# An fp32 decoder trunk on one core: weight splits ahead of the transposes' evacuations, modulation steps placed elsewhere

## The chip, the cores and the metric

The kernel runs on one core of a Trainium2 chip. The metric is the device time of one execution in microseconds (us), the median over several; less is better.

## The reference

`x` (1 x 256 x 1024, fp32) passes two layers, each of a half-step gated FFN, a token mixer and a second half-step FFN. Each of the six sub-layers is wrapped in norms and a modulation that is itself a product with the condition `c`. Cut to what matters here:

```
for layer in range(2):
    mod = (silu(c) @ ada_w[layer] + ada_b[layer]).reshape(B, 3, 3, D)
    h = rms_norm(x, g[0, 0]) * (1 + scale) + shift          # from mod
    y = (silu(h @ w_in[:, :2816]) * (h @ w_in[:, 2816:])) @ w_out
    x = x + 0.5 * gate * rms_norm(y, g[0, 1])
    y = short_conv(h') if layer == 0 else nsa(h', shared keys and values)
    x = x + gate' * rms_norm(y, g[1, 1])
    y = swiglu_ffn(h'', ...);  x = x + 0.5 * gate'' * rms_norm(y, g[2, 1])
```

The short convolution is three column parts of `h @ w_in`, two of them multiplied, convolved over three tokens, multiplied by the third, then a product with `w_out`. The attention has three branches (compressed, selected and window keys) in 16 heads; its keys and values come once from `x` after the first layer. All products keep fp32 accuracy.

## The kernel before, in words

**A product.** A matmul in full fp32 is replaced by three in a rounded fp32 form: a weight w is split into `whi` (its rounded copy) and `wlo = w - whi`, the activations likewise, and `mm3` (L252 to 254) adds x_hi w_hi, x_hi w_lo and x_lo w_hi. The activations stand transposed in `hx`, 8 blocks of 128 rows by 256 tokens, in a high and a low part; `t` is the half of 128 tokens. `prod(name, t)` multiplies one half of the tokens by 512 columns of a weight in 24 matmuls, and `prod_out` multiplies columns that were evacuated and transposed (`H`) by the second weight, into the `y` banks.

**Weights.** Every weight comes through a fixed plan (`w_init`) of transfers of 1 MB on SP's queue into three `raw` buffers. Each transfer holds two units of 128 x 1024. `fwd(n, g)` splits the next n units of the plan: first n copies on ACT (`whi`, L149), then on DVE n subtractions (`wlo`, L155) with g modulation steps pumped in between. Split units lie in pool A (6 buffers) or pool B (4), which the plan chooses by a letter. A raw buffer's next transfer is issued when its last subtraction is. Where a product needs a unit not yet split, `unit` splits it on the spot.

**Modulation.** 160 steps (`g_step`, L208) each multiply 512 KB of `ada_w`, which come by SP's queue into three `graw` buffers, with silu(c) on DVE and add them up into a column of `mod`. `pump` makes the credit for them, `g_need` forces those that a sub-layer needs next, and `row_of` turns a finished row for the gate with transposes (L304).

**Stages.** Start; first FFN; convolution; second FFN; keys' phase (`kv_side`); third FFN; attention (`nsa`, with `heads`); fourth FFN; end. Each FFN begins with `ffn_head` and then runs over blocks of 256 hidden columns. Between two sub-layers `turn_over` finishes the output product, adds to x (`z`, `x`), normalises, transposes (L290) and writes the new `hx` (L358 to 368). Meanwhile it runs the next sub-layer's first product in four pieces, p0 to p3 (`pair`, `kv_first`, `q_first`): the first half of the tokens needs only the first half of `hx`, and half two's transposes stand between p1 and p2.

**Order.** The engines' queues take what the program writes, in its order; no scheduler moves anything. A transposition is a TensorE instruction into a `tr` bank behind the product in hand, and its evacuation (ACT copies such as `quarter`, `H`, `T`; DVE's low part) waits for it. So where `fwd` stands in the text against an evacuation decides when its copies start.

## Time and profile before

| | us |
|---|---|
| median of 3 runs (1124.12 to 1126.97) | 1126.36 |
| the profiled execution, its own time | 1124.14 |
| its span in the profile | 1122.4 |
| TensorE busy | 1055.5 (94%) |
| DVE busy | 778.3 (69%) |
| ACT busy | 529.2 (47%) |
| mean granted clock of TensorE | 0.976 |

PE is TensorE's matmul, PEld its weight load, SP the engine whose queue issues transfers. In a timeline a row gives the start and length in us, the engine, the line, the operation, output <- inputs, the shape and a count; in brackets stands how long the engine had waited and for what. In a view of busy time by stage a row gives the stretch from:to and its length, then the busy us and the count of PE, PEld, DVE, ACT and POOL, then TensorE's granted clock (1.00 is full), the busy share of the DMA engines and the GB/s that they moved. The stretches are cut at the first matmul of each stage.

### The profile page before, as it was taken

Reading aid. Unit: us, or ns where it says so; the run is one execution under the profiler, and the core shown is the slowest. Engines: PE = TensorE matmul, PEld = TensorE weight load, DVE = VectorE, ACT = ScalarE, POOL = GpSimd, SP = SyncE. Lnnn points to the kernel's source line nnn. Section 1 sums busy time; section 2 is a strip of 40 time slices with the busy share of each in tenths; the row PEclk is TensorE's granted clock in tenths of the full one; section 3 lists DMA queues with packets and bytes.
Section 4 is the critical chain, followed back from the end, with each engine's and each line's share of the span. In section 5 each row is a group of like instructions: output and inputs, shape, how many; then the busy total and the mean of one; then the engine's idle time right before and its main releaser. Section 6 shows DMA issues by size and latency. Waiting matters only on the chain. (4 is left out here: it accounts for less than half of the span.)

```text
span 1122.4 us, 13355 instructions
## 1 busy us (share of the span) xinstructions
PE 1055.5 (94%) x4862; PEld 840.0 (75%) x4862; DVE 778.3 (69%) x1348; ACT 529.2 (47%) x974; POOL 31.4 (3%) x84
## 2 busy tenths in 40 slices
PE   5999999997999999999978999999999979999997
PEld 3578888775777888887857888886787757888786
DVE  5688788857675777777467877785477776665553
ACT  3444444645464344446444434444478645344342
POOL 0000000100010000001100000001000010000000
PEclk9999999999998999999999999999889989999999
DMA  9988988645645888885655888885411255655541
GB/s 367 389 300 298 344 314 327 236 163 215 224 167 187 314 294 308 288 292 211 225 205 209 314 308 300 290 304 199 177 63 39 94 206 201 236 222 184 188 150 38
DMA packets 51089, 263.50 MB, mean 235 GB/s; under 512 B 5584, under 2 KB 8016, under 8 KB 30288
## 3 DMA queue, kind: packets, MB, share of 16 engines
q1 hardware_dynamic: 50640, 261.61, 64.2%
q0 software_dynamic: 384, 1.05, 0.4%
q8 instruction: 38, 0.62, 0.2%
q14 instruction: 27, 0.22, 0.1%
HBM read 260.54 MB, written 1.05 MB: 233 GB/s over the span
## 5 line engine op out<-in xcount | busy, mean ns | idle before, releaser
L252 PE MATMUL in<-whiA,hx 128*128 128x512 f32 x760 | 300.6, 395 | 7.2 <-ACT whiA L149 3.6
L253 PE MATMUL in<-wloA,hx 128*128 128x512 f32 x760 | 298.5, 393 | 8.1 <-DVE wloA L155 8.1
L254 PE MATMUL in<-whiA,hx 128*128 128x512 f32 x760 | 299.4, 394 | 0.0
L155 DVE TENSOR_TENSOR wloA<-raw,whiA 128x1024 fp32r<-128x1024 f32 x205 | 246.0, 1219 | 68.4 <-ACT whiA L149 68.4
L149 ACT ACTIVATE whiA<-raw 128x1024 fp32r<-128x1024 f32 x205 | 205.7, 1049 | 12.9 <-DMA raw<-in_wi_dram 5.3
L208 DVE SCALAR_TENSOR_TENSOR graw<-graw,sc 128x1024 f32<-128x1024 f32 x147 | 178.8, 1218 | 4.8 <-DMA graw<-in_ada_dram 4.7
L252 PEld LDWEIGHTS in<-whiA,hx 128*128 128x128 f32 x760 | 143.5, 189 | 40.7 <-ACT whiA L149 5.5
L253 PEld LDWEIGHTS in<-wloA,hx 128*128 128x128 f32 x760 | 143.6, 189 | 39.4 <-DVE wloA L155 10.5
L254 PEld LDWEIGHTS in<-whiA,hx 128*128 128x128 f32 x760 | 143.5, 189 | 34.6 <-DVE hx L362 4.9
L422 ACT ACTIVATE sg<-in 128x256 f32<-128x256 f32 x86 | 33.0, 383 | 272.7 <-PE in L254 272.6
L252 PE MATMUL y<-whiB,H 128*128 128x512 f32 x368 | 152.2, 413 | 1.4 <-ACT whiB L149 1.4
L253 PE MATMUL y<-wloB,H 128*128 128x512 f32 x368 | 146.0, 397 | 3.4 <-DVE wloB L155 3.4
L155 DVE TENSOR_TENSOR wloB<-raw,whiB 128x1024 fp32r<-128x1024 f32 x112 | 134.2, 1221 | 21.0 <-ACT whiB L149 21.0
L254 PE MATMUL y<-whiB,H 128*128 128x512 f32 x368 | 146.1, 397 | 0.8 <-DVE H L296 0.8
L149 ACT ACTIVATE whiB<-raw 128x1024 fp32r<-128x1024 f32 x112 | 112.2, 1052 | 0.7 <-DMA raw<-in_wo_dram 0.4
L423 DVE TENSOR_TENSOR ht<-in,sg 128x256 f32<-128x256 f32 x86 | 36.4, 424 | 109.2 <-ACT sg L422 109.1
L253 PEld LDWEIGHTS y<-wloB,H 128*128 128x128 f32 x368 | 70.3, 191 | 17.6 <-DVE wloB L155 5.1
L254 PEld LDWEIGHTS y<-whiB,H 128*128 128x128 f32 x368 | 70.1, 190 | 17.0 <-DVE H L296 1.9
L252 PEld LDWEIGHTS y<-whiB,H 128*128 128x128 f32 x368 | 70.2, 191 | 13.8 <-ACT whiB L149 1.7
L295 ACT ACTIVATE H<-tr 128x256 fp32r<-128x256 f32 x88 | 33.1, 382 | 97.3 <-PE tr L290 97.3
L296 DVE TENSOR_TENSOR H<-tr,H 128x256 fp32r<-128x256 f32 x88 | 36.6, 420 | 44.8 <-ACT H L295 44.8
L290 PE MATMUL tr<-sm,ht 128*128 128x128 f32 x192 | 36.5, 276 | 7.2 <-DVE ht L423 5.1
(209 smaller groups left out, 1023.5 us busy)
## 6 DMA issues: line engine op xcount, KB each, us to landing
raw<-in_wi_dram SPq DMA_DIRECT2D x84, 1024.0 KB, 6.5
graw<-in_ada_dram SPq DMA_DIRECT2D x147, 512.0 KB, 4.8
raw<-in_wo_dram SPq DMA_DIRECT2D x44, 1024.0 KB, 6.9
raw<-in_cv_dram SPq DMA_DIRECT2D x12, 1024.0 KB, 6.4
whiB<-in_ada_dram SPq DMA_DIRECT2D x8, 512.0 KB, 9.7
raw<-in_ao_dram SPq DMA_DIRECT2D x4, 1024.0 KB, 5.6
raw<-in_q_dram SPq DMA_DIRECT2D x4, 1024.0 KB, 6.5
raw<-in_w_dram SPq DMA_DIRECT2D x4, 1024.0 KB, 6.9
```

Of the source, the lines that this page charges most:

```text
L149: nc.scalar.activation(hi[:, :w], raw, AF.Copy)
L155: nc.vector.tensor_sub(lo, raw, hi.bitcast(F32))
L208: self.nc.vector.scalar_tensor_tensor(w, w, 1.0, self.sc, op0=OP.mult, op1=OP.mult, accum_out=self.mod[:, m, k:k + 1])
L252: mm(out, xh, wh, start=start, stop=False, skip_group_check=True)
L253: mm(out, xh, wl, start=False, stop=False, skip_group_check=True)
L254: mm(out, xl, wh, start=False, stop=stop, skip_group_check=True)
L290: self.nc.tensor.transpose(o[:, i * 128:i * 128 + 128], src[:, i * 128:i * 128 + 128], self.ident)
L295: self.nc.scalar.activation(h[0], src, AF.Copy)
L296: self.nc.vector.tensor_sub(h[1], src, h[0].bitcast(F32))
L422: nc.scalar.activation(sg, o[:, 0:256], AF.Silu)
L423: nc.vector.tensor_mul(ht, o[:, 256:512], sg)
```

## The change

It does seven things. (1) In `conv`, `ffn_head`, `kv_side` and `kv_block` the call of `fwd` stands ahead of the evacuation of transposes (`then`, `turn_in`) instead of behind it; two `conv` blocks split 3 and 3 units instead of 2 and 4. (2) `ffn_head` pumps no modulation steps any more; the FFNs' rates rise to 1.5 (0.45 in the last), attention's rate falls from 3.0 to 1.5, `q_first` pumps 2 and 3 steps, and `nsa` pumps none at its start and more behind the heads. (3) The plan gives the second FFN's first output weight ahead of its third input block, and some units other pools. (4) In `pair` and `kv_first` one unit instead of two stands ahead of the second half's transposes. (5) The turn-over into the keys' phase splits 1 and 4 units in its middle, not 1 and 2. (6) In `heads` the query products of the third block stand ahead of the loop, those of the fourth at heads 2 and 3. (7) Two splits move from heads 8 and 9 to 12 and 14, and two others behind the gates and compressed values.

```diff
-    G_FFN = (1.5, 1.2, 1.25, 0.35)
+    G_FFN = (1.5, 1.5, 1.5, 0.45)
-    G_ATT = 3.0
+    G_ATT = 1.5
...
-        ffn(1, False, "ABAB")
+        ffn(1, False, "ABAA")
-        ffn(2, False)
+        ffn(2, False, "AABA")
-        ffn(3, False, "BAAB")
+        ffn(3, False, "BAAA")
...
@@ def pair(self, name, evac):
-            o[1] = self.prod((*name, 1), 0, None, range(2))
+            o[1] = self.prod((*name, 1), 0, None, range(1))
-            self.prod((*name, 1), 0, o[1], range(2, 4))
+            self.prod((*name, 1), 0, o[1], range(1, 4))
...
@@ def ffn_head(self, n):
         o = self.prod(("wi", n, 1), 1)
+        self.fwd(2)
         self.turn_in(ht[0, 1], H[0], 1)()
-        self.fwd(2, g)
         ht[1, 1] = self.evac_in(o)
...
@@ def conv(self, nxt):
         for j in range(2, 6):
             o = self.prod(("cv", j), 0)
+            self.fwd(3 if j in (2, 3) else 2, g)
             then[j - 1, 1]()
-            self.fwd(2, g)
             evac(j, 0, o)
             o = self.prod(("cv", j), 1)
+            self.fwd(3 if j in (2, 3) else 2, g)
             then[j, 0]()
-            self.fwd(4 if j in (2, 3) else 2, g)
             evac(j, 1, o)
...
@@ def kv_block(self, e):
         b = self.proj(("kw", e))
+        self.fwd(2)
@@ def kv_side(self, first):
         self.then[0]()
-        self.fwd(2, g)
+        self.pump(g)
         o = self.prod(("vv",), 1)
+        self.fwd(2)
         self.kv_evac(0, 1, o)
...
@@ def q_first(self):
             o[2] = self.compress(0)
+            self.pump(2)
...
             o[3]()
+            self.pump(3)
...
@@ def heads(self):
         self.cmp_scores(0)
+        self.q_half(2, 0)
         soft_a(0)
...
         scores(2)
+        self.q_half(2, 1)
         bias(3)
...
-            if i < 4:
-                self.q_half(2 + i // 2, i % 2)
+            if i in (2, 3):
+                self.q_half(3, i - 2)
...
-            if i < 4 or 8 <= i < 10:
+            if i < 4 or i in (12, 14):
                 self.fwd(1)
...
@@ def nsa(self, nxt):
         then()
-        self.fwd(2, g)
         gates()
         self.cmp_values()
+        self.fwd(2)
         self.heads()
...
-        self.fwd(4, g / 2)
+        self.fwd(4, g)
         self.prod_out(1, rows(0, 4), True, False)
-        self.fwd(2, g)
+        self.fwd(2, 2 * g)
@@ def run(self):
-        self.ffn(1, 8, over(self.kv_first, 19, 18))
+        self.ffn(1, 8, over(self.kv_first, 19, 18, more=(1, 4)))
```

Line numbers after the change are four to six lower for the same statement (L149 becomes L145, L155 becomes L151, L208 becomes L204).

ACT's queue in the convolution, around its third column block; `quarter<-tr` and `H<-quarter` evacuate transposes, `whiA` and `whiB` are weight copies. Before:

```order
L530 ACTIVATE sg<-in 128x256
L539 ACTIVATE quarter<-tr 128x2x128
L544 ACTIVATE z<-quarter,sm 128x256 x2
L149 ACTIVATE whiA<-raw 128x1024 x2
L552 ACTIVATE quarter<-in 128x512
L295 ACTIVATE H<-quarter 128x2x128 x2
L149 ACTIVATE whiB<-raw 128x1024 x2
L149 ACTIVATE whiA<-raw 128x1024 x2
```

After:

```order
L525 ACTIVATE sg<-in 128x256
L145 ACTIVATE whiA<-raw 128x1024 x2
L145 ACTIVATE whiB<-raw 128x1024
L534 ACTIVATE quarter<-tr 128x2x128
L539 ACTIVATE z<-quarter,sm 128x256 x2
L547 ACTIVATE quarter<-in 128x512
L145 ACTIVATE whiB<-raw 128x1024
L145 ACTIVATE whiA<-raw 128x1024 x2
L291 ACTIVATE H<-quarter 128x2x128 x2
```

The weight copies, three units per product instead of two and four, now stand ahead of the evacuation that needs the transposes.

ACT's queue in the head of the second FFN; `sg<-in` evacuates a product, `H<-tr` transposes. Before:

```order
L422 ACTIVATE sg<-in 128x256
L295 ACTIVATE H<-tr 128x2x128 x2
L149 ACTIVATE whiA<-raw 128x1024 x2
L422 ACTIVATE sg<-in 128x256
L295 ACTIVATE H<-tr 128x2x128
L149 ACTIVATE whiB<-raw 128x1024 x2
L422 ACTIVATE sg<-in 128x256
L295 ACTIVATE H<-tr 128x2x128
```

After:

```order
L418 ACTIVATE sg<-in 128x256
L145 ACTIVATE whiB<-raw 128x1024 x2
L291 ACTIVATE H<-tr 128x2x128 x2
L418 ACTIVATE sg<-in 128x256
L145 ACTIVATE whiA<-raw 128x1024 x2
L291 ACTIVATE H<-tr 128x2x128
L418 ACTIVATE sg<-in 128x256
L145 ACTIVATE whiA<-raw 128x1024 x2
L291 ACTIVATE H<-tr 128x2x128
```

The B copies that the first output product needs (`whiB`) moved from behind the second evacuated pair to the front, and each pair of copies ahead of its `H<-tr`.

DVE's queue behind attention, up to the turn-over's normalisation (`z<-x`); `graw` rows are modulation steps. Before:

```order
L155 TENSOR_TENSOR wloB<-raw,whiB 128x1024
L208 SCALAR_TENSOR_TENSOR graw,mod<-graw,sc 128x1024
L155 TENSOR_TENSOR wloB<-raw,whiB 128x1024
L208 SCALAR_TENSOR_TENSOR graw,mod<-graw,sc 128x1024 x3
L221 TENSOR_TENSOR mod<-mod,sm 128x8
L229 SCALAR_TENSOR_TENSOR mod<-mod,sm 128x8
L208 SCALAR_TENSOR_TENSOR graw,mod<-graw,sc 128x1024
L221 TENSOR_TENSOR mod<-mod,sm 128x8
L331 TENSOR_TENSOR z<-y,g 128x512 x2
L337 SCALAR_TENSOR_TENSOR x<-z,sty_7366,x 128x512 x2
L331 TENSOR_TENSOR z<-y,g 128x512
L345 TENSOR_SCALAR z<-x,stx_7401 128x512 x2
```

After:

```order
L151 TENSOR_TENSOR wloB<-raw,whiB 128x1024
L204 SCALAR_TENSOR_TENSOR graw,mod<-graw,sc 128x1024
L217 TENSOR_TENSOR mod<-mod,sm 128x8
L151 TENSOR_TENSOR wloB<-raw,whiB 128x1024
L204 SCALAR_TENSOR_TENSOR graw,mod<-graw,sc 128x1024 x2
L151 TENSOR_TENSOR wloB<-raw,whiB 128x1024
L327 TENSOR_TENSOR z<-y,g 128x512 x2
L333 SCALAR_TENSOR_TENSOR x<-z,sty_7372,x 128x512 x2
L327 TENSOR_TENSOR z<-y,g 128x512
L341 TENSOR_SCALAR z<-x,stx_7407 128x512 x2
```

Before, four forced steps stand directly ahead of the first `z<-y,g`, with the finishing of two rows (L221, L229) among them; now two pumped ones and a low half stand there, and the rows are finished earlier.

## Rows read from the trace of the kernel before

**Rows 1.** The page's busy shares, costliest groups (busy us, mean ns) and DMA issues

```profile
PE 1055.5 (94%) x4862; PEld 840.0 (75%) x4862; DVE 778.3 (69%) x1348; ACT 529.2 (47%) x974; POOL 31.4 (3%) x84
...
L155 DVE TENSOR_TENSOR wloA<-raw,whiA 128x1024 fp32r<-128x1024 f32 x205 | 246.0, 1219 | 68.4 <-ACT whiA L149 68.4
L149 ACT ACTIVATE whiA<-raw 128x1024 fp32r<-128x1024 f32 x205 | 205.7, 1049 | 12.9 <-DMA raw<-in_wi_dram 5.3
...
raw<-in_wi_dram SPq DMA_DIRECT2D x84, 1024.0 KB, 6.5
```

**Rows 2.** TensorE's timeline: start, length (us), instruction, count

```profile
74.27 0.39 PE L252 MATMUL in<-whiA,hx 128*128 128x512 f32 x1
...
79.72 0.39 PE L252 MATMUL in<-whiA,hx 128*128 128x512 f32 x1
...
327.08 1.07 PE L290 MATMUL tr<-sm,z 128*128 128x128 f32 x8
```

**Rows 3.** Busy time by stage; columns as told under the profile

```profile
74.27:204.16 129.89, 129.89 (x591) 106.96 (x590) 104.26 (x150) 55.33 (x77) 0.00 (x0) 1.00 0.88 322
...
230.65:315.58 84.93, 75.36 (x329) 59.55 (x328) 55.15 (x85) 41.18 (x66) 0.00 (x0) 0.96 0.55 196
341.34:364.90 23.56, 20.85 (x81) 16.22 (x80) 12.44 (x20) 8.89 (x15) 0.00 (x0) 0.86 0.47 164
364.90:511.77 146.87, 146.87 (x668) 120.78 (x666) 113.29 (x158) 63.78 (x89) 0.00 (x0) 1.00 0.85 301
...
525.70:586.88 61.18, 52.28 (x273) 41.95 (x274) 37.27 (x61) 32.41 (x62) 5.99 (x11) 0.98 0.54 188
586.88:609.67 22.79, 19.65 (x81) 15.52 (x80) 17.02 (x29) 9.49 (x15) 0.00 (x0) 0.90 0.50 174
...
804.95:887.26 82.31, 77.75 (x501) 63.53 (x501) 61.49 (x269) 58.39 (x198) 0.00 (x0) 0.88 0.20 71
...
910.05:934.15 24.10, 16.33 (x66) 12.47 (x65) 19.95 (x35) 17.64 (x38) 3.52 (x9) 0.86 0.39 143
934.15:953.80 19.65, 17.65 (x82) 14.18 (x81) 10.49 (x17) 8.62 (x15) 0.00 (x0) 1.00 0.44 156
```

**Rows 4.** The same view, stretches at half clock: first and last outside attention, then attention's

```profile
263.60:266.90 3.30, 3.30 (x9) 2.28 (x8) 1.67 (x3) 0.00 (x0) 0.00 (x0) 0.50 0.96 393
...
915.60:922.30 6.70, 5.37 (x16) 4.09 (x17) 4.90 (x12) 5.11 (x16) 1.76 (x6) 0.50 0.00 0
...
806.30:819.90 13.60, 12.77 (x53) 11.25 (x51) 13.41 (x55) 8.29 (x34) 0.00 (x0) 0.50 0.54 193
...
864.40:871.10 6.70, 6.60 (x26) 4.90 (x28) 4.68 (x18) 4.66 (x15) 0.00 (x0) 0.50 0.01 2
```

**Rows 5.** TensorE's timeline, convolution: waits for splits, first and last of five

```profile
247.80 0.50 PE L253 MATMUL in<-wloA,hx 128*128 128x512 f32 x1 [2.35 <-DVE wloA L155]
...
279.76 0.50 PE L253 MATMUL in<-wloA,hx 128*128 128x512 f32 x1 [2.29 <-DVE wloA L155]
```

**Rows 6.** ACT's timeline in the convolution

```profile
250.84 0.39 ACT L539 ACTIVATE quarter<-tr 128x256 f32<-128x256 f32 x1 [4.77 <-PE tr L290]
...
252.08 2.00 ACT L149 ACTIVATE whiA<-raw 128x1024 fp32r<-128x1024 f32 x2
```

**Rows 7.** TensorE's timeline, head of the second FFN

```profile
354.73 0.50 PE L252 MATMUL y<-whiB,H 128*128 128x512 f32 x1 [1.42 <-ACT whiB L149]
```

**Rows 8.** TensorE's timeline, keys' phase, first of eight waits for a split

```profile
540.12 0.38 PE L252 MATMUL in<-hx,whiB 128*128 128x256 f32 x1 [1.73 <-ACT whiB L149]
```

**Rows 9.** DVE's timeline behind attention

```profile
910.41 1.23 DVE L208 SCALAR_TENSOR_TENSOR graw<-graw,sc 128x1024 f32<-128x1024 f32 x1 [3.02 <-DMA graw<-in_ada_dram]
```

**Rows 10.** TensorE's timeline, turn-over behind attention

```profile
916.90 1.94 PE L290 MATMUL tr<-sm,z 128*128 128x128 f32 x8 [6.61 <-DVE z L345]
```

**Rows 11.** TensorE's timeline, modulation row of the last FFN

```profile
1056.60 1.06 PE L304 MATMUL tr<-sm,mod 128*128 128x128 f32 x8 [1.57 <-DVE mod L231]
```

**Rows 12.** TensorE's timeline, attention's heads

```profile
864.50 0.69 PE L290 MATMUL tr<-sm,small 128*128 128x128 f32 x2 [2.45 <-ACT T L953]
```

More of the change, by code (lines that the diff above doesn't have):

```diff
@@ L78, in ffn @@
                     wi(n, i // 2, i % 2, pools[i])
-                if n == 1:
-                    wi(n, 2, 0)
-                    wo(n, 0)
-                else:
-                    wo(n, 0)
-                    wi(n, 2, 0)
+                wo(n, 0)
+                wi(n, 2, 0)
                 wi(n, 2, 1)
@@ L456, in ffn_head @@
     def ffn_head(self, n):
-        g = self.G_FFN[n]
         ht = self.ht
@@ L571, in conv @@
         o = self.prod(("cv", 0), 1)
+        self.fwd(2, g)
         then[0, 0]()
         then[1, 0]()
-        self.fwd(2, g)
         evac(0, 1, o)
         o = self.prod(("cv", 1), 1)
+        self.fwd(2, g)
         then[0, 1]()
-        self.fwd(2, g)
         evac(1, 1, o)
@@ L581, in conv @@
             o = self.prod(("cv", j), 0)
+            self.fwd(3 if j in (2, 3) else 2, g)
             then[j - 1, 1]()
-            self.fwd(2, g)
             evac(j, 0, o)
             o = self.prod(("cv", j), 1)
+            self.fwd(3 if j in (2, 3) else 2, g)
             then[j, 0]()
-            self.fwd(4 if j in (2, 3) else 2, g)
             evac(j, 1, o)
@@ L592, in conv @@
         self.prod_out(0, rows(0, 4), True, False)
+        self.fwd(2, g)
         then[5, 1]()
-        self.fwd(2, g)
         self.prod_out(1, rows(0, 4), True, False)
@@ L641, in p1 @@
             self.kv_evac(0, 0, o[0])
-            o[1] = self.prod(("kk",), 0, None, range(2))
+            o[1] = self.prod(("kk",), 0, None, range(1))
         def p2():
-            self.prod(("kk",), 0, o[1], range(2, 4))
+            self.prod(("kk",), 0, o[1], range(1, 4))
         def p3():
             self.kv_evac(1, 0, o[1])
-            self.fwd(2)
         return p0, p1, p2, p3
@@ L670, in kv_side @@
         self.then[0]()
-        self.fwd(2, g)
+        self.pump(g)
         o = self.prod(("vv",), 1)
+        self.fwd(2)
         self.kv_evac(0, 1, o)
@@ L675, in kv_side @@
         T2.append(self.kv_block(1))
-        self.fwd(2, g)
         self.g_need(10)
@@ L684, in kv_side @@
         first[0]()
+        self.fwd(2)
         self.then[1]()
-        self.fwd(2)
         p = self.h_turned(1)
@@ L689, in kv_side @@
         self.h_split(1, p, 10, 9)
-        self.fwd(2)
         first[2]()
@@ L1028, in nsa @@
         then()
-        self.fwd(2, g)
         gates()
         self.cmp_values()
+        self.fwd(2)
         self.heads()
@@ L1037, in nsa @@
         self.prod_out(0, rows(0, 4), True, False)
-        self.fwd(4, g / 2)
+        self.fwd(4, g)
         self.prod_out(1, rows(0, 4), True, False)
-        self.fwd(2, g)
+        self.fwd(2, 2 * g)
         return nxt(rows(4, 8), None)
```

## The prediction

> **What bounds the kernel now.** I read first the page's busy shares and its costliest groups, then the windows by stage, then TensorE's waits in its timeline, and last what ACT and DVE did at those waits. TensorE is busy 94% of the span [rows 1], so nothing can be won inside its full stretches; what the reader is to look for is the other 6%. Beside TensorE the costly groups are the two halves of the weight split: ACT's high copy (1049 ns) and DVE's low subtraction (1219 ns) for each unit of weights [rows 1]. A full stretch shows what TensorE needs: from 74.27 to 79.72 us a product of 24 matmuls takes 5.45 us, 0.227 each; eight transposes take 1.07 us, 0.134 each [rows 2].
>
> The windows by stage tell where the idle time lies [rows 3]. The first FFN's steady stretch is TensorE without a gap at clock 1.00, although DVE is busy 80% of it (104.26 of 129.89 us) and the DMA queues move 322 GB/s. The second FFN has no gap either. The lost time is in the short stages between: convolution 84.93 us with 75.36 busy, head of the second FFN 23.56 with 20.85, keys' phase 61.18 with 52.28, head of the third FFN 22.79 with 19.65, turn-over behind attention 24.10 with 16.33. In all but the last DVE is busy 53 to 75% and ACT less, so they wait for order and not for capacity. The clock column adds a second loss, with 0.86 to 0.98 there. [...]
>
> In the convolution TensorE waits for splits: 2.35 us at 247.80 is the first and 2.29 at 279.76 the last of five [rows 5]. ACT's timeline shows why: at 250.84 it had waited 4.77 us for transposes which TensorE does only behind the product in hand, and the copies of the next weights, at 252.08, stand behind that wait [rows 6]. The changed order puts splits ahead, so that ACT and DVE work while TensorE multiplies.
>
> **The change part by part; gains against the profiled execution, 1124.14 us.**
>
> Convolution: eight products for the four later column blocks, two for the first ones and two output products of 24 are 288 matmuls x 0.227 = 65.4 us; 40 transposes x 0.134 are 5.4; TensorE's floor is 70.7. I add 1.3, half of one of today's waits, for evacuations that no order hides: 72.0, a gain of 12.9. Upper end 14.2, the floor itself. The lower end comes from DVE. Two products take TensorE 10.9 us. Where three units are split per product, DVE has six halves and 1.5 modulation steps in that time, 7.5 x 1.22 = 9.2, and about 2.5 of evacuations: it falls behind by 0.8 at each of two places, and if the clock halves there for a stretch like the first of [rows 4], each costs 0.8 + 1.65. That is 4.9, a gain of 8. I take the high side: over the stage DVE's 55.15 us are 77% of 72, less than the 80% that the first FFN bears without a gap [rows 3].
>
> [...]
>
> FFN heads: in each 72 matmuls are 16.3 us and 8 transposes 1.1, in all 17.4; with 0.3 for the first evacuation 17.7. Second FFN 23.56 - 17.7 = 5.9; its largest part is the wait of 1.42 for a high half [rows 7] and half of the 6.7 us at 0.50. Third 22.79 - 17.7 = 5.1; fourth 19.65 - 17.7 = 2.0, TensorE's idle time there [rows 3]. Modulation steps leave these stages too (eight, 1.22 us of DVE each). Together 13.0; ends 7.8 (only the idle time goes and no clock comes back: 2.7 + 3.1 + 2.0) and 13.8 (17.4 each).
>
> Keys' phase: six products of 24 (32.7 us), two blocks of 48 matmuls that are half as wide (96 x 0.114 = 10.9) and 24 transposes (3.2) give 46.8. Above it stand 14.4 us; the 1.73 waited for a high half at 540.12 is the first of eight waits for a split [rows 8]. A split now stands ahead of each product's evacuation, and three steps less are on DVE; but the second block's splits still follow the readers of the buffers that they fill. I leave 2.4 for that, 49.2, a gain of 12.0; ends 6 (half) and 14.4.
>
> Steps placed elsewhere: the 160 steps remain, 1.22 us on DVE and one transfer on SP's queue each. Seven more fall into the second FFN, six into the third, five into the turn-over behind the third. They raise a block pair from 3.6 or 3.75 steps to the 4.5 which the first FFN runs without a gap. DVE's share in the second FFN goes from 77% (113.29 of 146.87) to 83%, transfers to some 325 GB/s. Their cover is TensorE's own work and I cost them at nothing; if DVE were the bound there, the 13 steps would cost 16 us. The five stand ahead of query products that attention needs only later; nothing, at most 2.
>
> Turn-over behind attention: four forced steps stand on DVE between the output product and the normalisation, the last of them with a wait of 3.02 for its transfer [rows 9], and TensorE waits 6.61 for z [rows 10]. In the same place behind the convolution, without forced steps, the eight transposes have no wait [rows 2]. The steps alone are 4.9. I take 5.7, as the normalisation stays on the path for about 0.9; ends 4.9 and 6.6. The last FFN's modulation row waited 1.57 for its steps [rows 11]; they are done in time now: 1.6.
>
> Attention's heads: a wait of 2.45 behind a high copy [rows 12] and the 6.7 us at half clock that follow it [rows 4] go, since the two copies move to later heads: 2.45 + 3.35 = 5.8. Against it stand one of the two at its new place (1.05, the other hidden) and two that now stand right ahead of the first biases (2.1). That leaves 2.7, taken as 3. Query products ahead of the loop may fill some of the idle time by which the 13.6 us at half clock come about, up to 2, or lose 4, as their copy enters ACT's queue ahead of a bias that the third head awaits. Ends -3 and 8.
>
> Transposes after six instead of twelve matmuls: the second half's normalisation has 1.4 us less of cover, in five turn-overs. I take 0.4 in two, where nothing else fills it: -0.8; ends -2.8 (all of it in two) and 0.
>
> Sum: 12.9 + 13.0 + 12.0 + 5.7 + 1.6 + 3.0 - 0.8 = 47.4. The profiled execution becomes 1076.7. The median of the runs is 1126.36, 2.2 above it, so I predict **1079 us**. All low ends together give a gain of 20, all high ones 59; as terms don't fall to one end together, this case's own range is 1069 to 1091.
>
> **Rivals.** [...]
>
> Second, ACT becomes the bound in attention: 58.39 of 82.31 us is 71% already [rows 3], and query copies and splits in new places meet the exponentials. The stage takes 3 us more instead of 3 less, and its last splits come 2 late into the turn-over: gain 39, **1087**.
>
> Third, on the other side: weights do not land in time. In some 25 calls splits are asked for earlier, by up to the 4.77 us of [rows 6], while a transfer takes 6.5 [rows 1] and starts only when a raw buffer is free. A copy that waits holds the evacuation behind it, and TensorE idles. It decides from 47.4 / 25 = 1.9 us per call; with the 3.02 by which a step's transfer was late [rows 9], 25 x 3.02 = 75, less the gain: 1126 + 28 = **1154**. Against: with three buffers a transfer starts about three products, 16 us, ahead, and the first FFN takes 322 GB/s where the convolution moves 196.
>
> Fourth, the splits come no earlier, because the buffers that they fill are still read by the product in hand. Then only the work behind attention and the last row change, 7.3, and late splits take as much back in the turn-overs' new order: about **1124**.
>
> **Chances.** Forecast 0.66, first rival 0.18, second 0.09, third 0.04, fourth 0.03. The range that holds 8 in 10 takes in the forecast's own and the second rival, and reaches over the first: **1066 to 1099**, near the end of all high terms below. A measurement of this kernel can tell some 0.3% (3.4 us) from no change, as the three runs span 1124.12 to 1126.97. Only the fourth rival lies within that, only the third above: faster 0.93, same 0.03, slower 0.04.
>
> **What would show it.** Right: a convolution window near 72 us at clock 1.00 with no wait over 1.4 for a split; FFN heads near 17.7; keys' phase near 49; z transposes behind attention that don't wait for DVE; the last modulation row without a wait; FFN stretches still without gaps. Wrong: ACT's copies waiting for raw's transfer in the convolution, half-clock stretches outside attention, an attention window over 82, or longer FFN windows.

## The result, and the profile after

The changed kernel takes **1078.26 us** (median of 4, 1074.75 to 1083.93) against 1126.07 for the kernel before: a ratio of 0.9583 with a 95% interval of 0.9539 to 0.9626. Timed a second time, it gave 1077.36 against 1124.63, 0.9578 (0.9565 to 0.9592). The forecast was 1079, between 1066 and 1099. The profiled execution is the first of the four, 1074.75, with a span of 1073.0.

The page of the changed kernel, busy shares, costliest groups and the weight transfers (answers to [rows 1]):

```profile
PE 1034.8 (96%) x4862; PEld 829.0 (77%) x4862; DVE 776.7 (72%) x1348; ACT 530.5 (49%) x974; POOL 29.4 (3%) x84
...
L249 PE MATMUL in<-wloA,hx 128*128 128x512 f32 x776 | 303.3, 391 | 0.8 <-DVE wloA L151 0.8
L151 DVE TENSOR_TENSOR wloA<-raw,whiA 128x1024 fp32r<-128x1024 f32 (+1 forms) x209 | 250.4, 1218 | 48.6 <-ACT whiA L145 48.6
L145 ACT ACTIVATE whiA<-raw 128x1024 fp32r<-128x1024 f32 (+1 forms) x209 | 210.3, 1052 | 13.1 <-DMA raw<-in_wi_dram 4.6
...
raw<-in_wi_dram SPq DMA_DIRECT2D x84, 1024.0 KB, 6.7
```

No instruction became cheaper: split halves last 1052 and 1218 ns (1049 and 1219 before), DVE and ACT are within 2 us as long busy as before, the transfers land no faster. The row of L249 has the middle matmuls of a product, which need DVE's low half, for weights of pool A; behind its bar stands how long TensorE had waited for them. Before, the same row read:

```profile
L253 PE MATMUL in<-wloA,hx 128*128 128x512 f32 x760 | 298.5, 393 | 8.1 <-DVE wloA L155 8.1
```

So this wait fell from 8.1 to 0.8 us. In all, TensorE's idle time fell by 28.7 us (66.9 to 38.2) and its busy time by 20.7 (1055.5 to 1034.8, the same 4862 matmuls at a mean clock of 0.992 instead of 0.976): together the 49.4 us by which the span is shorter.

The same by stage (answers to [rows 3]; columns as told under the profile before):

```profile
74.28:204.16 129.88, 129.88 (x591) 106.96 (x590) 104.72 (x152) 55.40 (x77) 0.00 (x0) 1.00 0.88 322
230.31:301.09 70.78, 70.74 (x330) 57.75 (x328) 55.69 (x84) 41.34 (x65) 0.00 (x0) 1.00 0.70 255
326.95:344.33 17.38, 17.38 (x82) 14.25 (x80) 11.52 (x17) 9.96 (x15) 0.00 (x0) 1.00 0.48 167
344.33:491.21 146.88, 146.88 (x668) 120.78 (x666) 117.37 (x166) 62.40 (x87) 0.00 (x0) 1.00 0.88 318
505.64:554.39 48.75, 48.49 (x273) 41.38 (x273) 33.47 (x53) 32.72 (x62) 6.00 (x11) 1.00 0.62 216
554.39:571.76 17.37, 17.37 (x81) 14.26 (x80) 14.64 (x24) 9.95 (x15) 0.00 (x0) 1.00 0.40 129
...
753.16:848.40 95.24, 86.13 (x584) 70.77 (x583) 62.44 (x281) 62.90 (x206) 0.00 (x0) 0.95 0.21 78
...
872.36:888.93 16.57, 14.57 (x56) 10.69 (x57) 14.57 (x25) 14.42 (x28) 1.32 (x4) 0.90 0.50 188
888.93:906.36 17.43, 17.43 (x81) 14.25 (x80) 10.90 (x15) 9.96 (x15) 0.00 (x0) 1.00 0.38 130
```

Convolution, keys' phase and the three FFN heads are now TensorE with hardly a gap (0.26 us in the keys' phase, 0.04 or none in the others), at clock 1.00. The FFN stretches are unchanged to 0.01 us, although DVE is 4.1 us busier in the second one. The largest piece of idle time that is left, 9.1 us, lies in attention (95.24 us, clock 0.95); 2.0 lie behind it, in the first product of the last FFN (16.57 us, 0.90).

### The profile page after: what moved, and what is told of

Its sections match the earlier page's. It is cut to its first block, busy times and chain, and to the rows that moved or that the text cites. A ratio compares the mean times of both kernels' runs of the same rounds, so it can differ in the third digit from the quotient of the medians.

```text
span 1073.0 us, 13377 instructions
## 1 busy us (share of the span) xinstructions
PE 1034.8 (96%) x4862; PEld 829.0 (77%) x4862; DVE 776.7 (72%) x1348; ACT 530.5 (49%) x974; POOL 29.4 (3%) x84
## 3 DMA queue, kind: packets, MB, share of 16 engines
q0 software_dynamic: 384, 1.05, 0.4%
HBM read 260.54 MB, written 1.05 MB: 244 GB/s over the span
## 5 line engine op out<-in xcount | busy, mean ns | idle before, releaser
L248 PE MATMUL in<-whiA,hx 128*128 128x512 f32 x776 | 305.6, 394 | 3.5 <-ACT hx L355 1.8
L250 PE MATMUL in<-whiA,hx 128*128 128x512 f32 x776 | 304.8, 393 | 0.0
L249 PE MATMUL in<-wloA,hx 128*128 128x512 f32 x776 | 303.3, 391 | 0.8 <-DVE wloA L151 0.8
L151 DVE TENSOR_TENSOR wloA<-raw,whiA 128x1024 fp32r<-128x1024 f32 (+1 forms) x209 | 250.4, 1218 | 48.6 <-ACT whiA L145 48.6
L145 ACT ACTIVATE whiA<-raw 128x1024 fp32r<-128x1024 f32 (+1 forms) x209 | 210.3, 1052 | 13.1 <-DMA raw<-in_wi_dram 4.6
L204 DVE SCALAR_TENSOR_TENSOR graw<-graw,sc 128x1024 f32<-128x1024 f32 x147 | 178.8, 1218 | 0.6 <-DMA graw<-in_ada_dram 0.6
L250 PEld LDWEIGHTS in<-whiA,hx 128*128 128x128 f32 x776 | 146.0, 188 | 35.3 <-DVE hx L358 4.9
L248 PEld LDWEIGHTS in<-whiA,hx 128*128 128x128 f32 x776 | 146.0, 188 | 35.0 <-ACT hx L355 2.8
L249 PEld LDWEIGHTS in<-wloA,hx 128*128 128x128 f32 x776 | 146.2, 188 | 31.0 <-DVE wloA L151 1.4
L248 PE MATMUL y<-whiB,H 128*128 128x512 f32 x368 | 150.6, 409 | 0.0
L249 PE MATMUL y<-wloB,H 128*128 128x512 f32 x368 | 144.3, 392 | 2.1 <-DVE wloB L151 2.1
L250 PE MATMUL y<-whiB,H 128*128 128x512 f32 x368 | 144.6, 393 | 0.9 <-DVE H L292 0.9
L151 DVE TENSOR_TENSOR wloB<-raw,whiB 128x1024 fp32r<-128x1024 f32 x108 | 129.4, 1221 | 13.8 <-ACT whiB L145 13.8
L145 ACT ACTIVATE whiB<-raw 128x1024 fp32r<-128x1024 f32 x108 | 108.5, 1054 | 4.6 <-PE in L249 2.8
L249 PEld LDWEIGHTS y<-wloB,H 128*128 128x128 f32 x368 | 69.4, 189 | 15.7 <-DVE wloB L151 3.3
```

Source lines behind the costliest of these rows:

```text
L145: nc.scalar.activation(hi[:, :w], raw, AF.Copy)
L151: nc.vector.tensor_sub(lo, raw, hi.bitcast(F32))
L204: self.nc.vector.scalar_tensor_tensor(w, w, 1.0, self.sc, op0=OP.mult, op1=OP.mult, accum_out=self.mod[:, m, k:k + 1])
L248: mm(out, xh, wh, start=start, stop=False, skip_group_check=True)
L249: mm(out, xh, wl, start=False, stop=False, skip_group_check=True)
L250: mm(out, xl, wh, start=False, stop=stop, skip_group_check=True)
```

## The experiments

Two theories stood against each other from the start. **Order**: TensorE waited because splits stood behind evacuations in ACT's and DVE's queues. **Load**: it waited because modulation steps and splits were too much for DVE in these stages, and taking steps away was the cure.

### The convolution's order alone

The kernel before, with only the convolution's method of the change:

```diff
             o = self.prod(("cv", j), 0)
+            self.fwd(3 if j in (2, 3) else 2, g)
             then[j - 1, 1]()
-            self.fwd(2, g)
             evac(j, 0, o)
             o = self.prod(("cv", j), 1)
+            self.fwd(3 if j in (2, 3) else 2, g)
             then[j, 0]()
-            self.fwd(4 if j in (2, 3) else 2, g)
```

(and the same move in the three other places of the method)

> The kernel before with only the convolution's method of the change (splits ahead of the evacuations, 3 and 3 units). Theory 'order': the splits that TensorE waited for are made while it multiplies, whatever the other edits do. The convolution's window falls from 84.93 to 71 to 72 us, its waits for splits go, the run takes 13 to 14 us less, about 1112. Rival 'load': the stage needs the pools and step places of the other edits too; then the window stays above 78 and the run above 1119.

Measured: 1108.54 us (4 runs) against 1123.42, ratio 0.9881 (0.9854 to 0.9908). Its convolution:

```profile
230.60:301.34 70.74, 70.70 (x330) 57.76 (x328) 56.48 (x86) 41.58 (x66) 0.00 (x0) 1.00 0.71 254
```

70.74 us with the old pools and the old places of the steps, and with as much DVE work as before (56.48 against 55.15 us): the order does it alone (with 3 and 3 units per product for 2 and 4, which was not run by itself). Load is out for this stage.

### The FFN heads' splits behind again

```diff
         o = self.prod(("wi", n, 0), 1)
-        self.fwd(2)
         for b in range(2):
             self.turn_in(ht[b, 0], H[b], 0)()
+        self.fwd(2)
```

(all three places, still without steps)

> The changed kernel with the FFN heads' splits behind the transposes' evacuations again, still without modulation steps in them. Theory 'order': the three heads, now 17.38, 17.37 and 17.43 us, lose again what the late copies cost; the second FFN's goes to 21 to 23.5 with a wait for a split of over 1 us, the others 1 to 3 us up; 5 to 10 us in all. Rival 'load': the steps that left the heads were the cost; then all three stay within 0.5 us of 17.4.

Measured: 1080.96 us (one run). The three heads, in order:

```profile
328.46:347.48 19.02, 17.54 (x81) 14.18 (x80) 9.22 (x14) 8.32 (x14) 0.00 (x0) 1.00 0.39 135
...
556.73:575.76 19.03, 17.56 (x82) 14.18 (x81) 12.62 (x21) 8.33 (x14) 0.00 (x0) 1.00 0.28 98
...
893.24:912.34 19.10, 17.62 (x82) 14.18 (x81) 8.62 (x13) 8.32 (x14) 0.00 (x0) 1.00 0.28 99
```

Each is 1.64 to 1.67 us longer, 4.97 together, just under the range of the theory, and the second FFN's head does not go back to 21. The one wait left in each shows in TensorE's timeline:

```profile
344.48 0.41 PE L286 MATMUL tr<-sm,ht 128*128 128x128 f32 x2 [1.48 <-DVE ht L419]
```

DVE's `ht` stands behind low halves whose copies came late. So without steps the order is worth 1.65 us per head, and the rest of what the heads gained (6.18, 5.42 and 2.22 less 1.65 each) has other causes. For it the next run was made.

### Steps in the FFN heads, splits still ahead

```diff
+        g = self.G_FFN[n]
         o = self.prod(("wi", n, 0), 1)
-        self.fwd(2)
+        self.fwd(2, g)
```

(all three places)

> The changed kernel with modulation steps pumped in the FFN heads again (1.5 per call, more than before), the splits still ahead of the evacuations. With splits behind and no steps the heads were 19.0 each, and with splits behind and steps 20.9 to 22.3 (in the run of the convolution alone). Theory: with the splits ahead DVE has room, 11 to 15 us busy of 17.4, and three to five steps fit; the second and third FFN's heads stay under 18. Rival: the steps delay low halves or ht whatever the order; each head 1.5 to 3.5 us longer.

Measured: 1079.19 us (one run). Heads of the second and third FFN:

```profile
328.41:345.78 17.37, 17.37 (x81) 14.25 (x80) 15.22 (x23) 9.95 (x15) 0.00 (x0) 1.00 0.71 240
...
555.41:573.56 18.15, 17.56 (x81) 14.18 (x80) 17.47 (x30) 9.95 (x15) 0.00 (x0) 1.00 0.51 179
```

With splits ahead, four more steps cost the first one nothing (DVE 15.22 us of 17.37), and three more cost the second one 0.78, a little past the 18 of the theory; DVE is busy 17.47 of 18.15 there and is full. With splits behind and steps, the same two heads took 22.26 and 20.89 in the run of the convolution alone, and 23.56 and 22.79 with the same code in the kernel before [rows 3]. (The difference of 1.3 and 1.9 between these two is TensorE's busy time at clocks of 0.92 and 1.00 against 0.86 and 0.90.) So neither alone is the cause: with splits ahead steps are nearly free, without steps a split behind costs 1.65, and the two together cost 3.5 to 6.2. (Both kernels with the old heads also have the old plan, in which the second FFN's first output weight comes later; how much of that head's 4.9 to 6.2 us is the plan's was not taken apart. In the third FFN the plan differs in the pools alone.)

### No early steps ahead of attention

```diff
             o[2] = self.compress(0)
-            self.pump(2)
...
             o[3]()
-            self.pump(3)
```

> The changed kernel without the five modulation steps that it pumps in the turn-over into attention, so that later ones are forced again. Theory: three forced steps stand ahead of the normalisation behind attention; the z transposes wait 3 to 6 us for DVE (0.20 in the changed kernel), and the last FFN's modulation row waits 1.5 to 3; together 5 to 9 us more. Rival: the normalisation's own chain set the 6.61 us before; then both waits stay under 1 us and the time is the same.

Measured: 1075.52 us (one run), no longer than the changed kernel's 1075 to 1084. In its timelines, DVE's forced steps and TensorE's wait:

```profile
863.39 1.23 DVE L204 SCALAR_TENSOR_TENSOR graw<-graw,sc 128x1024 f32<-128x1024 f32 x1 [2.19 <-DMA graw<-in_ada_dram]
...
867.55 1.28 DVE L327 TENSOR_TENSOR z<-y,g 128x512 f32<-128x512 f32 x2
```

```profile
872.69 1.07 PE L286 MATMUL tr<-sm,z 128*128 128x128 f32 x8 [2.65 <-DVE z L341]
```

In the changed kernel the same row reads:

```profile
870.84 1.06 PE L286 MATMUL tr<-sm,z 128*128 128x128 f32 x8 [0.20 <-DVE z L341]
```

Three steps are forced here, and the wait is 2.65: less than the 3 to 6 expected, more than the rival's 1. Why it is less can be read from two kernels. In this run `z` starts 8.75 us after the first matmul of that output product (867.55 - 858.80), in the kernel before 12.71 us (right behind the step of [rows 9], 911.76 - 899.05). The difference, 3.96, is exactly that of the waits, 6.61 - 2.65. So `z` may start 6.1 us behind that matmul at no cost, as TensorE has the second half's matmuls to do, and between these two kernels every microsecond beyond that counts. What went past this cover in the kernel before was mostly transfers: the last step had waited 3.02 us for its own [rows 9], and one of the three before it 1.40:

```profile
903.23 1.23 DVE L208 SCALAR_TENSOR_TENSOR graw<-graw,sc 128x1024 f32<-128x1024 f32 x1 [1.40 <-DMA graw<-in_ada_dram]
```

Together they are 4.4 of the 6.61 us; without them the wait would have been some 2.2 (an estimate, 6.61 - 4.42). The second wait that was expected, of the modulation row, did not come; the last FFN's higher rate may have made up for the steps. And the 2.45 us more of waiting were half given back: the next product, which in the changed kernel waits on the spot for two splits, took 15.20 instead of 16.57.

### Two units ahead of the second half's transposes

```diff
-            o[1] = self.prod((*name, 1), 0, None, range(1))
+            o[1] = self.prod((*name, 1), 0, None, range(2))
...
-            self.prod((*name, 1), 0, o[1], range(1, 4))
+            self.prod((*name, 1), 0, o[1], range(2, 4))
```

(keys' phase alike)

> The changed kernel with two units instead of one ahead of the second half's transposes, as before. The prediction's term: this edit costs 0.8 us, so undoing it wins 0.8 in the turn-overs. Rival: with the splits early the second half's hx is what the next product awaits, so that undoing it costs 0.5 to 1 us in each place where the second half ends late, above all in the keys' phase (48.75 us now). Rival two: nothing, within 0.3 us in each window.

Measured: 1075.55 us (one run). The turn-over into the second FFN takes 25.71 us instead of 25.86, the keys' phase 48.73 instead of 48.75, and the first product behind attention to the head 16.75 instead of 16.57. The turn-over into the keys' phase took 161.00 us together with the second FFN ahead of it, instead of 161.31; with the same code there, other executions took 160.55 to 161.70. Nothing that can be told from noise: this part of the change does not matter.

### Transfers asked for late in the convolution

```diff
-                self.w_dma(i + 1 + self.RAW)
+                self.w_dma(i + 1 + (1 if self.plan[i][1][0][0] in ("cv", "ao") else self.RAW))
```

> The changed kernel with the weight transfers of the convolution asked for one half ahead instead of three. It prices the third rival of the prediction. A half then takes its landing of 6.4 us, two high copies and a low half, some 9.7 us, where TensorE needs 5.45 for the product that uses it: 4.2 us of waiting for each of 12 to 14 halves, the window of 70.78 us goes to 120 to 135, with ACT's copies waiting for raw's transfer and the evacuations late behind them. If transfers had little to do with it, the window would stay under 80.

Measured: 1100.24 us (one run). The convolution, and ACT's timeline in it:

```profile
231.50:316.53 85.03, 75.48 (x329) 60.78 (x328) 55.05 (x83) 40.02 (x63) 0.00 (x0) 0.94 0.48 188
```

```profile
255.24 2.01 ACT L145 ACTIVATE whiA<-raw 128x1024 fp32r<-128x1024 f32 x2 [3.14 <-DMA raw<-in_cv_dram]
260.47 0.73 ACT L291 ACTIVATE H<-quarter 128x256 fp32r<-128x256 f32 x2 [3.22 <-DVE quarter L551]
...
264.75 2.01 ACT L145 ACTIVATE whiA<-raw 128x1024 fp32r<-128x1024 f32 x2 [3.07 <-DMA raw<-in_cv_dram]
267.22 1.06 ACT L145 ACTIVATE whiB<-raw 128x1024 fp32r<-128x1024 f32 x1 [0.46 <-DMA raw<-in_ao_dram]
```

The mechanism is as the third rival had it: copies wait 3.14 us for a transfer, and the evacuation in the row below is late behind them (it waits for DVE's `quarter`, which stands behind their low halves). The size was far off: 14.3 us more in the window and 4.3 in the turn-over behind it, where 50 to 65 were expected. The expectation counted one landing per half, one after the other. SP's queue shows three transfers asked for within 1 us:

```profile
259.15 0.38 SPq L130 DMA_DIRECT2D raw<-in_cv_dram  x1
259.62 0.38 SPq L130 DMA_DIRECT2D raw<-in_ao_dram  x1
260.11 0.37 SPq L130 DMA_DIRECT2D raw<-in_cv_dram  x1
```

The copies that waited for the first two of them started at 264.75 and 267.22, 2.5 us apart, where a single landing in this stage takes 5.5 to 7.4 us (medians): the landings overlap instead of following one another.

So with one half of lead instead of three, late weights take back all that this stage gained: 85.03 us against 84.93 before, and 30.18 against 25.76 in the turn-over behind it. Of the whole gain of 48 us that is 18.6, so that lateness in this stage alone could not have made the change slower. No lead at all was not run. In the changed kernel itself no copy in the convolution waits for a transfer.

### Attention: query products in the loop, splits at heads 8 and 9

```diff
-        self.q_half(2, 0)
         soft_a(0)
...
-            if i in (2, 3):
-                self.q_half(3, i - 2)
+            if i < 4:
+                self.q_half(2 + i // 2, i % 2)
```

> The changed kernel with all four query products in the loop over the heads again, as before. The prediction's term: their place ahead of the loop wins up to 2 us of the idle time at the start of the heads; undone, attention from its first product to the first output product (95.24 us) goes to 96 to 97.5. Rival: their copy enters ACT's queue ahead of a bias that a head awaits, and costs; undone, the stage goes to 91 to 94. Rival two: within 0.5 us.

and, in a kernel of its own,

```diff
-            if i < 4 or i in (12, 14):
+            if i < 4 or 8 <= i < 10:
                 self.fwd(1)
```

> The changed kernel with the last two splits of the heads at heads 8 and 9 again instead of 12 and 14. The prediction's term: behind the high copy there TensorE waited 2.45 us and then ran 6.7 us at half clock; undone, attention's stage of 95.24 us gets 2 to 6 us longer. Rival: the stall only moved along with the splits (a half-clock stretch stands near 840 in the changed kernel); undone, the stage stays within 1 us.

Measured: 1074.31 and 1081.31 us (one run each), attention 93.99 and 100.62. As times these looked like an answer, and are none. The same stage with the very same code in two of the other experiments, and in each the three microseconds that begin 15 us into it:

```profile
753.31:848.88 95.57, 86.52 (x584) 71.23 (x583) 62.53 (x281) 62.59 (x206) 0.00 (x0) 0.95 0.21 78
...
768.31:771.31 3.00, 3.00 (x26) 2.88 (x25) 3.00 (x6) 0.66 (x4) 0.00 (x0) 1.00 0.00 0
```

```profile
773.02:873.31 100.29, 91.21 (x584) 75.61 (x583) 62.53 (x281) 62.60 (x206) 0.00 (x0) 0.90 0.20 74
...
788.02:791.02 3.00, 3.00 (x13) 2.59 (x13) 3.00 (x6) 0.66 (x4) 0.00 (x0) 0.50 0.00 0
```

(two units first; transfers late.) With the work identical, one execution has a clock of 0.95 and the other of 0.90, and they differ by 4.7 us. So a single execution cannot tell a move of 2 us here: by their times, both runs are inconclusive.

TensorE's waits tell more, because they come back from execution to execution. The changed kernel's attention has three over 1 us:

```profile
787.58 0.45 PE L946 MATMUL tr<-sm,small 128*128 128x128 f32 x1 [3.30 <-DVE small L939]
...
824.57 0.44 PE L286 MATMUL tr<-sm,small 128*128 128x128 f32 x2 [1.54 <-ACT T L949]
...
839.86 0.30 PE L946 MATMUL tr<-sm,small 128*128 128x128 f32 x1 [3.12 <-DVE small L939]
```

In four executions of this code they were 3.29 to 3.30, 1.50 to 1.54 and 3.10 to 3.12 us. With the query products in the loop again the first is gone and the other two stay; its row:

```profile
789.45 0.33 PE L946 MATMUL tr<-sm,small 128*128 128x128 f32 x1
```

So the query products ahead of the loop brought this wait. It stands behind the low half of head 0, which the kernel before has too, but there TensorE had a query product to do meanwhile. With the splits at heads 8 and 9 again the first wait stays at 3.29, and the others read:

```profile
831.66 0.44 PE L286 MATMUL tr<-sm,small 128*128 128x128 f32 x2 [2.46 <-ACT T L949]
...
848.19 0.33 PE L946 MATMUL tr<-sm,small 128*128 128x128 f32 x1 [1.85 <-ACT T L949]
```

That is 2.46 and 1.85 us in place of 1.54 and 3.12: the splits' new place exchanged waits and won nothing.

### The changed kernel again

> The changed kernel itself, unaltered, timed beside the others. In the runs so far attention, whose code was the same, took 94.4 to 100.3 us; theory: the clock falls at the start of the heads in some executions and not in others, so single executions spread over 1074 to 1084 as before, and 1078 is their middle.

Measured: 1077.36 us (4 runs, 1075.93 to 1078.62), attention 97.66 at 0.91 in the profiled one. Over six executions of the changed attention (95.24, 95.44, 95.57, 97.66, 97.69, 100.29; the second with two modulation steps more) the middle is 96.6, against 96.17 and 96.01 in two of the old one. The gain of 3 us that the prediction put there is not to be seen.

### Splits earlier still

The rest of the idle time invited the same rule again. In the product behind attention, TensorE of the changed kernel waits for splits made on the spot:

```profile
877.27 0.49 PE L248 MATMUL in<-whiA,hx 128*128 128x512 f32 x1 [1.23 <-ACT whiA L145]
878.53 0.79 PE L249 MATMUL in<-wloA,hx 128*128 128x512 f32 x1 [0.77 <-DVE wloA L151]
```

and in the heads, in the row at 787.58 above, for a low half that stands ahead of a softmax's scaling on DVE.

```diff
         o = self.prod(("q0",), 1)
+        self.fwd(2)
         self.then()
...
         gates = self.gates()
+        self.fwd(2)
         self.cmp_keys()
...
         self.cmp_values()
-        self.fwd(2)
...
-            if i < 4 or i in (12, 14):
+            if i in (2, 3, 12, 14):
...
-        self.fwd(2, 2 * g)
+        self.fwd(4, 1.0)
```

(and the last FFN's step rate 0.6 instead of 0.45)

> The changed kernel with four splits earlier by the same rule: the two for the third query block under the first query product of attention, the two for the fourth under the gates' evacuation, the third and fourth unit of the last FFN's first weight behind the output product instead of on the spot, with one step there instead of three; the two splits of heads 0 and 1 are thereby free. Theory 'order': the spot splits' waits of 1.23 and 0.77 go and the half clock behind them, so that from the first product of the last FFN to its head it takes 13 instead of 16.57; attention 95.24 goes to 90 to 93; the run 1069 to 1073. Rival: the copies wait for buffers and hold evacuations; both stages stay or get longer, 1078 or more.

Measured: 1081.33 us (4 runs), ratio 0.9614 (0.9599 to 0.9630): worse than the changed kernel. Half of the theory held: the product behind attention takes 12.81 us at clock 1.00, 3.8 less. But attention took 105.42, at a clock of 0.87:

```profile
754.72:860.14 105.42, 94.28 (x584) 77.42 (x583) 63.05 (x281) 63.02 (x206) 0.00 (x0) 0.87 0.19 70
...
884.09:896.90 12.81, 12.79 (x56) 9.55 (x57) 11.56 (x23) 12.43 (x26) 1.34 (x4) 1.00 0.33 113
```

DVE's and TensorE's timelines name the place:

```profile
766.26 2.36 DVE L151 TENSOR_TENSOR wloA<-raw,whiA 128x1024 fp32r<-128x1024 f32 x2 [4.01 <-ACT whiA L145]
...
768.80 0.39 DVE L737 COPY KC<-tr 64x30 f32<-64x30 f32 x2
```

```profile
769.94 1.97 PE L754 MATMUL tr<-w,rep 128*128 128x64 f32 x8 [1.91 <-DVE rep L746]
```

The two splits behind the gates wait on DVE for ACT's copies, which stand behind the gates' evacuation and so wait for the gates' product, and the compressed keys' copies (KC, rep), which had been ready to run, queue behind them. TensorE idles 1.91 us there, and 2.00 before it for ACT; behind these two waits its clock was 0.50 or 0.51 from 769.72 to 781.72. Here a split ahead, with copies behind it that were ready to run, became a loss: 4.01 us of DVE's queue stood still.

Next, the splits inside the heads were taken apart, the high copy behind the transposes' copies, the low half at the head's end:

```diff
             trans(i)
+            lows = self.fwd(1, late=True) if i in (2, 3, 12, 14) else None
...
-            if i in (2, 3, 12, 14):
-                self.fwd(1)
+            if lows:
+                lows()
```

(with `late`, `fwd` makes its high copies and returns the low halves as a call of its own)

> The one before with the four splits inside the heads taken apart: the high copy on ACT right behind the copies of the transposes that TensorE waits for, the low half on DVE at the end of the head. Theory: TensorE's waits behind high copies in the heads go, as ACT waits for DVE at that point anyway; attention 1 to 3 us shorter than with whole splits, without a half-clock stretch near its middle. Rival: ACT is full in the heads and the copy delays the exponentials instead; within 1 us or longer.

Measured: 1078.71 us (5 runs), 0.9582 (0.9568 to 0.9597); attention 102.26, at a clock of 0.88. That is 3.2 us less than the one before in single executions, and 2.6 less in the medians, with the two splits behind the gates still in it. Of the later heads' waits over 1 us, 1.51 and 3.11 in the one before, one of 1.79 is left, as the theory had it; but a stretch at half clock still stands near the middle (0.50 from 820.56 to 823.56).

Last, the four query splits go under the first query product, where ACT and DVE wait for TensorE; against the kernel just above nothing else differs:

```diff
         o = self.prod(("q0",), 1)
-        self.fwd(2)
+        self.fwd(4)
         self.then()
...
         gates = self.gates()
-        self.fwd(2)
         self.cmp_keys()
```

> The changed kernel with all four splits of the third and fourth query block under attention's first query product, where ACT and DVE have nothing to do, none ahead of the compressed keys (the place at which two of them held DVE up for 4 us in the run before last), none at heads 0 and 1, the other four in the heads with the high copy behind the transposes' copies and the low half at the head's end; the last FFN's first weight split behind the output product, with one step there. Theory: the first softmax starts some 2 us earlier, the wait of 3.3 us at the second head goes, and attention takes 90 to 93 us instead of 95.2 to 97.7; from the last FFN's first product to its head 12.8 instead of 16.6; the run 1066 to 1071. Rival: the clock falls at the start of the heads all the same, attention stays at 97 or more and the run at 1074 or above.

Measured: **1067.97 us** (5 runs, 1066.76 to 1072.69), ratio 0.9507 (0.9487 to 0.9526), clear of the changed kernel's 0.9578. It is the fastest version here. DVE in that place, then the two stages:

```profile
754.78 5.26 DVE L153 TENSOR_TENSOR wloA<-raw,whiA 128x1024 fp32r<-128x1024 f32 x4 [0.45 <-ACT whiA L145]
759.96 0.28 DVE L730 COPY hT<-tr 128x120 f32<-128x120 f32 x1
```

```profile
753.31:844.00 90.69, 84.83 (x583) 70.32 (x583) 62.85 (x281) 63.02 (x206) 0.00 (x0) 0.96 0.20 77
...
867.95:880.76 12.81, 12.81 (x56) 9.56 (x57) 11.56 (x23) 12.44 (x26) 1.34 (x4) 1.00 0.34 111
```

The four low halves end at 760.0, just where the next copy (hT) can start: it starts 6.65 us into the stage, in the changed kernel 6.48. Attention takes 90.69 and the product 12.81. The wait at the second head did not go, as the theory had it, but fell to 2.15 us, although no split stands ahead of it any more.

This pair prices the place behind the gates, since only two splits moved between them. The kernel just above has in the same stage

```profile
754.56:856.82 102.26, 93.20 (x584) 77.15 (x583) 64.32 (x283) 63.04 (x206) 0.00 (x0) 0.88 0.19 71
```

so that attention is 11.6 us shorter in the profiled executions, and the run 10.7 in the medians (1078.71 to 1067.97), or 8.4 by the ratios to the kernel before (0.9582 to 0.9507), whose intervals are clear of each other. TensorE's idle time fell by 3.2 us (9.06 to 5.86), its busy time by 8.4: most of what the place cost was half clock behind its two waits (0.50 from 772.56 to 781.56 in the kernel just above, where this one has 1.00 from the stage's start to 783.31).

## Why the prediction was right, point by point

| term | predicted gain | measured in the profile |
|---|---|---|
| convolution | 12.9 | 84.93 to 70.78: 14.2 |
| three FFN heads | 13.0 | 6.2 + 5.4 + 2.2 = 13.8 |
| keys' phase | 12.0 | 61.18 to 48.75: 12.4 |
| turn-over behind attention | 5.7 | 35.10 to 29.52 (from the last output product to the head): 5.6 |
| last modulation row | 1.6 | its wait of 1.57 is gone |
| attention | 3.0 | 96.17 to 95.24: 0.9, and none over several executions |
| transposes a unit earlier | -0.8 | two turn-overs together -0.6; undone, nothing |
| not forecast | 0 | turn-over into the convolution 0.3, third FFN with the turn-over into attention 0.8, rest of the last FFN 0.4: 1.5 |
| sum | 47.4 | 1122.4 to 1073.0: 49.4 |

The mechanism was right, and so were the sizes of its large terms; that the median came out within 1 us of the forecast is luck. Executions of the changed kernel spread over 9 us, and attention's 2.1 us too much were made up by the convolution, the heads and the 1.5 us that nobody had forecast.

**The floors were right.** The convolution, the FFN heads and the keys' phase ended within 2 us of the matmul counts times 0.227 us [rows 2]. The 1.3 us that the prediction left above the convolution's floor was not needed: the window is the upper end of its range. The choice between the ends (order against DVE's capacity) was settled by the run of the convolution alone: 70.74 us with the old load.

**The keys' phase has the right size, and no run takes it apart.** In the kernel before, the eight waits for a split [rows 8] are 7.2 us together, and the changed kernel has none of them. That the order removed them, and not the three steps that left or the four units that are now split in the turn-over ahead, is argued from the convolution and the heads and not shown. The pools were not tried by themselves either.

**The cause named for the FFN heads was only part of it.** The prediction put waits behind late copies first, with the 6.7 us at clock 0.50 beside them (355.80 to 362.50, in the rows under the rivals below), and named the steps that leave in passing. The runs show 1.65 us per head for the order by itself, 0 and 0.8 for steps by themselves, and that the rest is order and steps on DVE together (in the second FFN the plan may have its part).

**Behind attention** the size held (5.6 against 5.7), by a different sum: the z transposes' wait fell by 6.41 and the stretch that ends with them by 6.87 (19.82 to 12.95; its clock rose from 0.92 to 1.00), and 1.29 were given back in the product behind them (15.28 to 16.57 us), which now meets two splits on the spot and behind them a mean clock of 0.74 (the last row of this section). The step "The steps alone are 4.9" was right in place and not in kind: `z` may start 6.1 us behind the first matmul at no cost, and 4.4 of the 6.61 us past that were waits for the steps' transfers.

**The failed term is attention's 3.0.** The stall behind the high copy [rows 12] was to go, and shrank from 2.45 to 1.54 us (the row at 824.57). The split that moved to head 12 was costed at 1.05, the length of its copy; it brought the wait of 3.12 at 839.86, because on DVE its low half stood in front of the softmax's scaling:

```profile
837.88 1.23 DVE L151 TENSOR_TENSOR wloA<-raw,whiA 128x1024 fp32r<-128x1024 f32 x1 [2.25 <-ACT whiA L145]
```

So the prediction costed the moved splits by their own length and left out who queues behind them on DVE. And the query products ahead of the loop, which were to fill up to 2 us of idle time or to lose up to 4 behind their copy on ACT, brought the wait of 3.30 at 787.58 behind a low half that had not moved, and with it a stretch with a mean clock of 0.56:

```profile
785.30:791.90 6.60, 4.32 (x20) 4.14 (x21) 4.18 (x17) 3.82 (x13) 0.00 (x0) 0.56 0.02 4
```

**The costs set at nothing were nothing.** The second FFN's stretch is 146.88 against 146.87 us. DVE is at 80% there and not at the predicted 83%: six more steps came in, and three low halves went out, into the head ahead of it. The third FFN with the turn-over into attention, where the five steps went, is 181.40 us against 182.21.

**The rivals.** The first, to which the chances give 0.18, was half clock as before in the stretches outside attention. The kernel before has six of them, 26.6 us together; two are in [rows 4], the other four read:

```profile
280.70:284.00 3.30, 3.30 (x10) 2.42 (x9) 0.47 (x2) 0.00 (x0) 0.00 (x0) 0.50 0.91 278
355.80:362.50 6.70, 5.98 (x15) 4.67 (x16) 2.17 (x4) 0.55 (x3) 0.00 (x0) 0.50 0.87 303
584.50:587.80 3.30, 3.30 (x10) 2.54 (x9) 0.27 (x1) 0.38 (x1) 0.00 (x0) 0.50 0.76 258
605.00:608.30 3.30, 3.05 (x9) 2.50 (x10) 1.52 (x3) 2.36 (x4) 0.00 (x0) 0.50 0.83 278
```

In the second of these four a matmul came every 0.43 us (357.12 to 360.96), where a full stretch has 0.227. The rival is out in five of the six places, where the clock is now 1.00. In the sixth, behind attention, a sign of being wrong came true in part: behind the two splits on the spot the mean clock is 0.74, which is some 1.7 us lost there (an estimate, a quarter of 6.6):

```profile
877.80:884.40 6.60, 5.87 (x22) 4.74 (x22) 6.60 (x8) 5.83 (x7) 0.00 (x0) 0.74 0.56 202
```

The second (ACT bound in attention) did not come: ACT is busy 62.90 us of 95.24, and was 62.86 of 96.17. The third has no sign in the changed kernel's convolution; the run with late transfers prices it there at 18.6 us with one half of lead. The fourth is out by the first experiment.

## What to carry to other kernels

Count TensorE's floor for each stage (matmuls times the pitch of a full stretch) and compare it with the window: where no other engine is near full, look for order first. In the convolution it was had whole by putting work for the next product ahead of evacuations that wait for this one; in attention, where DVE and ACT are busy two thirds of the time, the same rule won nothing (95.24 and 97.66 us against 96) until the splits stood where nothing waits behind them (90.69). Before moving an instruction ahead in ACT's or DVE's queue, ask what its own input waits for and what stands ready behind it (a wait of 4.01 us stood ahead of the ready KC copies here): under a product whose result nobody needs yet it was all but free, and in front of ready copies two splits cost some 8 to 11 us here (attention 102.26 against 90.69). Behind attention, late work on DVE cost nothing up to 6.1 us here, and from there one for one (3.96 us later, 3.96 us more of waiting).

## What the runs showed that was not expected

TensorE's clock need not fall at the same place in two executions of the same code. Attention with identical instructions took 95.57 us at a mean granted clock of 0.95 and 100.29 at 0.90, while the keys' phase was 48.73 us in both. That is half of the changed kernel's spread of 1074.75 to 1083.93, and a stage with short idle times must be compared over several executions, or by its waits, which came back to 0.04 us while the work was the same.

Cutting the lead of the weight transfers from three halves to one cost 18.6 us instead of 50 to 65. The rows say why: three transfers were asked for within 1 us, and the copies of the first two started 2.5 us apart, where one landing takes 5.5 to 7.4.
